# Sliding-window attention with value products on column halves, in an order written out by hand

## The chip, the cores and the metric

The kernel runs on one core of one Trainium2 chip. The metric is the device time of one execution in microseconds, as the median of several runs. The profile comes from one further execution with the hardware profiler on. The engines are named as the profile names them: PE (TensorE, matmuls), PEld (its weight loads), DVE (VectorE), ACT (ScalarE), POOL (GpSimd), and SP (SyncE, which only issues transfers).

## The reference

One step of a two-layer encoder on 2048 prompt tokens and 32 sample tokens, in float32. Layer A is a gated delta rule with eight heads. From its output x one shared K and V (4 heads of 64) are projected. Layer B is attention in chunks of 64 tokens: each chunk reads its own keys and those of the two chunks before it, 16 query heads in groups of four share one K/V head, and a learned sink takes part in the softmax.

```
q = rope(x @ w_q) * 64**-0.5 ;  z = x @ w_z
s = q . k                                   # own chunk and two back, <= 192 keys
m = max(s.max(-1), sink)
p = exp(s - m) ;  p = p / (p.sum(-1) + exp(sink - m))
out = (p @ v * silu(z)) @ w_out             # 1024 x 1024
y = layer_norm(ALPHA * x + out)
```

The 32 sample tokens read a cache of 128 keys and their own 32 in the same way. The change touches layer B's attention and what stands just before it.

## The kernel before

The program runs through layer A, then through `P2`, the projection of x onto K, V, Q and the gate z, then through `Attention`. What matters here is P2 and the attention.

**P2.** Weights were split beforehand into a high and a low part, and a product is three matmuls for each of four slices of 128 rows (`product`, L1291 to L1293), 12 matmuls of 416 columns. Ten units (V, K, and four each of Q and z) are worked on three spans of tokens: tokens 0 to 415 in the plain way, four products per unit (`plain`), and two spans of 832 tokens with seven Winograd-like products per unit (`winograd`, reading tiles named xs). `units` is a generator that yields after each product, and `sequence` fixes the order of units. Weights come through a ring of 12 tiles (`load`, L1273, issued from ACT's queue); `load` is called after each product and fills the ring again. Splitting the sums of x for a span (`load_pair`, L1189, L1194, L1215) is interleaved with plain units: `both` takes two pieces of the split for each product. What follows a product (tanh gate for z, rope for Q and K, transposition for V) is queued in `todo` and worked off later by `after`.

**Attention, per chunk of 64 tokens** (`chunk`), for each of two pairs of K/V heads (p = 0, 1):

- Scores, L1624: four f32 matmuls. Two heads share the 128 partitions, 64 each, so a matmul uses only 64 rows of the array, the lower or the upper.
- Softmax: maximum on DVE (L1499, L1500, L1508), four exponentials with their sums on ACT (L1507, L1509), reciprocal on DVE (L1510, L1511), scaling on POOL (L1632). The scaled sets lie with two heads side by side for each key chunk.
- Turning, L1639: six transposes through PE into tiles tr, copied back by ACT (L1641) and DVE (L1643) as pt.
- Values, L1645: three matmuls of 256 columns. The stationary operand is vd, the values of one chunk for two heads on a block diagonal, half of it zeros. The result is multiplied by the gate (L1648).

vd is loaded from memory in four pieces for each stretch of chunks (L1488), around memsets on POOL (L1486). Two chunks make a tile of 128 tokens, whose output projection and norm are `finish`: 48 matmuls of 512 columns (L1532 to L1534), layer norm on DVE, ACT and POOL. Chunks go in the order 10 to 31, then 0 to 9, and the sample last (`sample`).

**What sets the order.** P2 up to the last Winograd unit stands in a block in which PE, DVE, ACT and POOL work in the order written. Attention stands outside it: there the planner of the language orders all engines by its own estimate of costs. The last four plain units are given out with the first four chunks, and 16 pieces of output weights are loaded afterwards by `open_right`, when the memory of P2 is free.

Of the kernel before, what the change touches and what calls it, by code (L numbers as in the profile page):

```python
# [1134 lines left out]
class P2:  # L1135
# [10 lines left out]
    def __init__(self, tc, right, mid, I, O, T, G):  # L1146
        self.tc, self.nc, self.I, self.O, self.T, self.G = tc, tc.nc, I, O, T, G
        self.res = new_pool(tc, right, "p2_res", 1, side="right")
        self.wp = new_pool(tc, right, "p2_w", self.RING, side="right")
# [3 lines left out]
        self.ppl = None  # L1153
        self.turn = 0
        self.todo, self.second, self.staged = [], [], []
# [3 lines left out]
    def load_right(self):  # L1159
# [20 lines left out]
        for t, c in zip(self.cs0, ("cos", "sin")):  # L1180
            nc.sync.dma_start(t[:], self.I[c][:, 0:TB])

# [83 lines left out]
    def load(self, most=2):  # L1266

        for _ in range(most):
            if self.loads and len(self.held) < self.RING:
                what, slot = self.loads.pop(0)  # L1270
                w = self.wp.tile([128, 2, 4, 128], F32R, tag="w", name="w")
                src = self.T["w2"][UNITS.index(what[:2]), SLOTS.index(slot)]
                self.nc.scalar.dma_start(w[:].rearrange("p s k c -> p s (k c)").bitcast(F32), src)  # L1273
# [10 lines left out]
    def spare(self):  # L1284
        return self.wk.tile([128, 4, 128], F32, tag="hT", name="hT", bufs=2)

    def product(self, ps, w, x, first, last):
        nc = self.nc
        for k in range(4):
# [5 lines left out]
    def units(self, units):  # L1295

        self.loads = [(u, s) for u in units for s in self.slots(u)]
        self.held = []
# [20 lines left out]
    def plain(self, unit):  # L1319
# [3 lines left out]
        for c in range(2):  # L1323
            ps = (self.ppl or self.ppr).tile([128, 512], F32, tag="ps", name="ps")[:, :TB]
            for h in range(2):
                self.product(ps, self.weight(unit, self.PLAIN[c][h]), x[4 * h:4 * h + 4], h == 0, h == 1)
# [111 lines left out]
class Attention:  # L1438


    def __init__(self, tc, left, I, O, T, G):
# [9 lines left out]
        self.turn = 0  # L1451
# [3 lines left out]
        self.nsk = one.tile([128, 8], F32, tag="nsk", name="nsk")  # L1455
        self.sks = one.tile([128, 4], F32, tag="sks", name="sks")
        for i in range(2):
            nc.sync.dma_start(self.nsk[i * 64:i * 64 + 64, :], I["sinks"][i].partition_broadcast(64))
        for i in range(4):
            nc.sync.dma_start(self.sks[i * 32:i * 32 + 32, :], I["sinks_s"][i].partition_broadcast(32))  # L1460
        V.tensor_scalar(out=self.nsk[:], in0=self.nsk[:], scalar1=-1.0, scalar2=None, op0=ALU.mult)
        V.tensor_scalar(out=self.sks[:], in0=self.sks[:], scalar1=-1.0, scalar2=None, op0=ALU.mult)
        self.pend = []
        self.data = {}

    def open_right(self, right):
        tc, I = self.tc, self.I
        R = "right"
        self.oone = new_pool(tc, right, "u_one", 1, side=R)
        self.otwo = new_pool(tc, right, "u_two", 2, side=R)  # L1470
        self.pp = new_pool(tc, right, "u_pp", 1, PSUM, side=R)
        self.ps_s.append(new_pool(tc, right, "u_ps", 1, PSUM, side=R))
        rest = load_out_weights(self.nc, self.oone, self.T["wo"][1], self.nc.sync)
        self.w = next(rest)
        drain(rest)

    def tables(self):
        self.tabs = ln_tables(self.nc, self.oone, self.I["b_ln_g"], self.I["b_ln_b"])

    def load_kv(self, a, z):  # L1480
        nc, T = self.nc, self.T
        nc.sync.dma_start(self.kT[:, :, a * 64:z * 64], T["bk"][:, :, a * 64:z * 64].rearrange("a p t -> p a t"))
        src = T["bv"][0:NP, :].rearrange("(c k) (p d) -> k c p d", k=64, p=2)
        for i in range(2):
            rows, off = slice(i * 64, i * 64 + 64), slice(64 - i * 64, 128 - i * 64)
            nc.gpsimd.memset(self.vd[rows, a:z, :, off], 0.0)  # L1486
            for p in range(2):
                nc.sync.dma_start(self.vd[rows, a:z, p, rows], src[:, a:z, p, rows])  # L1488

    def scores_tile(self):  # L1490
        self.turn += 1
        return self.ps_s[self.turn % len(self.ps_s)].tile([128, 2, 2, 256], F32, tag="S", name="S")

    def softmax(self, S, P, nskc):

        nc, V, thr = self.nc, self.nc.vector, self.thr
        nsub = len(P)
        nm = thr.tile([128, 4], F32, tag="nm", name="nm")
        V.tensor_reduce(out=nm[:, :nsub], in_=S, axis=AX.X, op=ALU.max, negate=True)  # L1499
        V.tensor_tensor(out=nm[:, :nsub], in0=nm[:, :nsub], in1=nskc, op=ALU.min)  # L1500
        sm = thr.tile([128, 4], F32, tag="sm", name="sm")
        es_ = thr.tile([128, 4], F32, tag="es", name="es")
        for u in range(nsub):
            src = S[:, u, :]
            if len(P[u].shape) == 3:
                src = src.rearrange("r (j k) -> r j k", k=64)
            nc.scalar.activation(P[u], src, AF.Exp, bias=nm[:, u:u + 1], scale=1.0, accum_out=sm[:, u:u + 1])  # L1507
# [428 lines left out]
```

## Time and profile before

| | us |
|---|---|
| median of 3 runs | 2197.37 |
| range of the runs | 2195.75 to 2205.4 |
| the profiled execution | 2203.02 |
| its span, first to last instruction | 2201.2 |
| PE busy | 2103.0 (96%) |
| DVE busy | 1490.1 (68%) |
| ACT busy | 911.1 (41%) |
| POOL busy | 713.5 (32%) |

Times inside the profile are microseconds from the start of the span. The attention begins near 1762 and takes the rest. A row of the timeline gives start, length, engine, line, operation, operands and count; starts are measured, while the ends of matmuls are modelled, so the cost of a matmul in a stream is read from one start to the next. Stretches list for each engine its busy time and its count of instructions.

### The profile page before, as it was taken

The numbers are of one execution on the slowest core, as the hardware profiler recorded it, in microseconds if no ns is written. First come the engines' busy times: TensorE is split into PE (matmuls) and PEld (weight loads), VectorE is DVE, ScalarE is ACT, GpSimd is POOL, SyncE is SP. The second block draws the span as 40 slices with busy tenths as digits, with TensorE's granted clock in tenths as the row PEclk, the third lists the DMA queues.
The fourth block names the chain that finished last, engine by engine and source line by source line (L and its number), as shares of the span: only waits on it lengthen the run. The fifth ranks groups of instructions, "written<-read, shape, count | busy, mean of one in ns | idle before, by whom it ended". The sixth has DMA issues, their size and how long they took to land.

```text
span 2201.2 us, 37188 instructions
## 1 busy us (share of the span) xinstructions
PE 2103.0 (96%) x13370; PEld 1911.1 (87%) x13370; DVE 1490.1 (68%) x2771; ACT 911.1 (41%) x2405; POOL 713.5 (32%) x1176
## 2 busy tenths in 40 slices
PE   8999999999989999998889999899899988999997
PEld 6999999999989889887778888899899976888775
DVE  5888977876657589888865665555835566556663
ACT  5545545544422477667742111311311034444441
POOL 1212211161111188788841210000000025565653
PEclk9999999999999999999999999999999999999999
DMA  7656656567764645545735766888788895333321
GB/s 283 224 186 192 223 172 195 175 191 242 243 212 161 204 131 163 153 147 180 235 105 179 255 218 243 298 278 284 266 285 285 273 305 135 100 83 96 96 73 43
DMA packets 348377, 430.00 MB, mean 195 GB/s; under 512 B 78352, under 2 KB 276080, under 8 KB 348176
## 3 DMA queue, kind: packets, MB, share of 16 engines
q1 hardware_dynamic: 311856, 311.07, 44.5%
q10 hardware_dynamic: 36336, 116.55, 15.8%
q8 instruction: 106, 1.74, 0.3%
q14 instruction: 79, 0.65, 0.1%
HBM read 269.45 MB, written 158.44 MB: 194 GB/s over the span
## 4 chain that ended last, share of the span: by engine, by line
PE 77%; DVE 9%; POOL 5%; ACT 4%; DMA 3%; issue 2%; ACTq 0%; SPq 0%; POOLq 0%; DVEq 0%
PE ps L77 10%; PE ps L79 10%; PE ps L78 10%; PE ps L1291 5%; PE ps L1292 5%; PE ps L1293 5%; PE ot L1645 3%; PE po L1052 3%; PE po L1054 3%; PE po L1053 3%; PE po L1532 3%; PE po L1533 3%; PE po L1534 3%; PE S L1624 2%; POOL Tt L588 2%
## 5 line engine op out<-in xcount | busy, mean ns | idle before, releaser
L77 PE MATMUL ps<-act_hi,w_hi 128*128 128x416 f32 x1280 | 458.7, 358 | 6.4 <-DVE z L322 2.7
L79 PE MATMUL ps<-act_hi,w_lo 128*128 128x416 f32 x1280 | 450.5, 353 | 5.0 <-POOL w_lo L54 3.2
L78 PE MATMUL ps<-act_lo,w_hi 128*128 128x416 f32 x1280 | 451.3, 353 | 0.0
L77 PEld LDWEIGHTS ps<-act_hi,w_hi 128*128 128x128 f32 x1280 | 241.8, 189 | 11.0 <-DVE z L322 3.1
L79 PEld LDWEIGHTS ps<-act_hi,w_lo 128*128 128x128 f32 x1280 | 242.0, 189 | 9.8 <-POOL w_lo L54 4.3
L78 PEld LDWEIGHTS ps<-act_lo,w_hi 128*128 128x128 f32 x1280 | 242.6, 190 | 2.8
L1291 PE MATMUL ps<-xs_h,w 128*128 128x416 f32 x560 | 199.6, 356 | 11.4 <-DVE ra L1348 7.1
L1292 PE MATMUL ps<-xs_l,w 128*128 128x416 f32 x560 | 199.9, 357 | 3.1 <-DVE xs_l L1194 3.1
L1293 PE MATMUL ps<-xs_h,w 128*128 128x416 f32 x560 | 198.4, 354 | 0.0
L54 POOL TENSOR_TENSOR w_lo<-w_raw,w_hi 128x1024 fp32r<-128x1024 f32 x32 | 80.5, 2516 | 357.3 <-ACT w_hi L53 343.3
L295 DVE SCALAR_TENSOR_TENSOR y<-R,convw,y 128x2083 f32<-128x2083 f32 (+2 forms) x78 | 175.1, 2245 | 24.8 <-ACT y L293 24.6
L585 POOL TENSOR_TENSOR tm<-L,Tt 128x60 f32<-128x60 f32 (+19 forms) x375 | 136.3, 363 | 87.9 <-DVE L L572 49.9
L588 POOL TENSOR_TENSOR Tt<-Tt,tm 128x60 f32<-128x60 f32 (+19 forms) x375 | 143.6, 383 | 28.3
L1632 POOL TENSOR_TENSOR P<-P,sm 128x384 f32<-128x384 f32 (+2 forms) x128 | 100.9, 810 | 119.1 <-DVE sm L1511 56.5
L1486 POOL MEMSET vd<- 64x768 f32 (+2 forms) x10 | 7.8, 778 | 397.0 <-DVE ra L1348 396.7
L1507 ACT ACTIVATE P<-S,nm 128x192 f32<-128x192 f32 (+2 forms) x260 | 104.6, 419 | 61.1 <-DVE nm L1500 52.3
L1291 PEld LDWEIGHTS ps<-xs_h,w 128*128 128x128 f32 x560 | 106.4, 190 | 14.6 <-DVE ra L1348 7.8
L1348 DVE SCALAR_TENSOR_TENSOR ra<-ps,u 128x416 f32<-128x416 f32 x60 | 35.4, 590 | 122.3 <-PE ps L1293 121.4
L1052 PE MATMUL po<-wo,g_hi 128*128 128x512 f32 (+1 forms) x272 | 110.7, 407 | 0.9 <-DVE hT L1100 0.9
L1292 PEld LDWEIGHTS ps<-xs_l,w 128*128 128x128 f32 x560 | 106.2, 190 | 5.6 <-DVE xs_l L1194 4.2
L1293 PEld LDWEIGHTS ps<-xs_h,w 128*128 128x128 f32 x560 | 106.9, 191 | 1.2
L95 ACT CAST pre_hl<-pre_raw 128x256 fp32r<-128x256 f32 x184 | 65.7, 404 | 101.6 <-DMA pre_raw<-in_b_w_z 25.8
(298 smaller groups left out, 4799.8 us busy)
## 6 DMA issues: line engine op xcount, KB each, us to landing
w<-s_w ACTq DMA_DIRECT2D x180, 512.0 KB, 4.6
s_w<-pre_hl SPq DMA_DIRECT2D x160, 256.0 KB, 2.5
w_raw<-in_w_in SPq DMA_DIRECT2D x32, 512.0 KB, 6.5
s_wo<-pre_hl SPq DMA_DIRECT2D x64, 256.0 KB, 4.1
gb<-s_gcum SPq DMA_DIRECT2D x34, 256.0 KB, 5.2
k<-s_k SPq DMA_DIRECT2D x34, 256.0 KB, 4.0
s_z<-z SPq DMA_DIRECT2D x40, 208.0 KB, 2.1
s_q<-y SPq DMA_DIRECT2D x8, 1024.0 KB, 5.2
```

The source lines that it names most:

```text
L77: nc.tensor.matmul(ps, hi[:, k, :], xh[:, k, :], start=(k == 0), stop=False)
L78: nc.tensor.matmul(ps, hi[:, k, :], xl[:, k, :], start=False, stop=False)
L79: nc.tensor.matmul(ps, lo[:, k, :], xh[:, k, :], start=False, stop=(k == KC - 1))
L295: self.nc.vector.scalar_tensor_tensor(out=y[:, a:z], in0=R[:, a + j:z + j], scalar=self.convw[:, i, j:j + 1], in1=y[:, a:z], op0=ALU.mult, ...
L585: P.tensor_tensor(out=tm[:n, i0 - k:, :w], in0=L[:n, i0:, j:j + 1].to_broadcast(sh), in1=Tt[:n, j:j + 1, :w].to_broadcast(sh), op=ALU.mult)
L588: P.tensor_tensor(out=Tt[:n, i0:, :w], in0=Tt[:n, i0:, :w], in1=tm[:n, i0 - k:, :w], op=ALU.subtract)
L1052: nc.tensor.matmul(ps[:n], ghi[:, k, :n], w[0][k][:, cs], start=(k == 0), stop=False)
L1291: nc.tensor.matmul(ps, w[:, 0, k], xh[:], start=first and k == 0, stop=False, skip_group_check=True)
L1292: nc.tensor.matmul(ps, w[:, 0, k], xl[:], start=False, stop=False, skip_group_check=True)
L1293: nc.tensor.matmul(ps, w[:, 1, k], xh[:], start=False, stop=last and k == 3, skip_group_check=True)
L1507: nc.scalar.activation(P[u], src, AF.Exp, bias=nm[:, u:u + 1], scale=1.0, accum_out=sm[:, u:u + 1])
L1632: nc.gpsimd.tensor_tensor(out=P[:, u, :nj], in0=P[:, u, :nj], in1=f.unsqueeze(1).unsqueeze(3).to_broadcast([128, nj, 2, 64]), op=ALU.mult)
```

## The change

The pieces of `chunk` become methods that are called one by one, in an order written out by hand for PE, DVE and ACT (POOL and SP stay with the planner):

- `scores(n)`: all eight score matmuls of a chunk, then both maxima. `exps`, `norm`, `turn`, `values` are the other steps.
- For `norm` and `turn`, the keys of a chunk are a pair (two chunks that lie together in 128 partitions of the new tile vp) and a single chunk. The sets of a pair are turned as four blocks of 128 keys, one for each query pair and head; the single's two heads lie side by side in P1 and are turned together.
- `values`: for the pair, two matmuls with 64 stationary columns, one for each head, into the lower and the upper 64 output partitions; for the single, two more with the halves of vd. Four matmuls of 256 columns for each head pair, where there were three.
- `beside(n)`: scores of chunk n, then turning of the chunk before it between quarters of a half tile of output projection, then that chunk's values. `first` does it for the first chunk after P2, and `opening` for the first four, between halves of the plain products (`fine`).
- The sample stands between chunk 31 and chunk 0, as one step of this order.
- vp is loaded in one transfer per stretch; the diagonal blocks of vd are copied from it by POOL.
- The ring of weights moves to a place of its own that outlives P2. After the last projection weights it takes 12 of the 16 output weight pieces; four are loaded as before.
- Keys of chunks 8 to 11 (kTa), queries of chunks 10 to 13 and the sinks are loaded during P2 into a place of their own.
- In the sequence of P2 units, z 3 for tokens 0 to 415 moves ahead of the first Winograd span (ten plain products there instead of six), and V for these tokens moves ahead of the second span. Three plain units instead of four are left beside the attention.
- The last tile is stored in halves on two queues. The norm of a tile is issued within the next tile's projection. A buffer for turned rows of layer A's output shares the tag rs.

```diff
     def __init__(self, tc, ring, right, mid, I, O, T, G):
+        self.wp = new_pool(tc, ring, "p2_w", self.RING, side="right")
+        self.kp = new_pool(tc, ring, "p2_keep", 1, side="right")
...
+    def first_keys(self):
+        src = self.T["bk"][:, :, 512:768].rearrange("a p t -> p a t")
+        self.nc.sync.dma_start(self.keep[1][:], src)
+        self.queries(10)
+        self.queries(12)
...
     def spare(self):
-        return self.wk.tile([128, 4, 128], F32, tag="hT", name="hT", bufs=2)
+        return self.wk.tile([128, 4, 128], F32, tag="rs", name="hT")
...
-        self.loads = [(u, s) for u in units for s in self.slots(u)]
+        self.loads = [(u, s) for u in units for s in self.slots(u)] + [(None, i) for i in range(self.RING)]
...
 class Attention:
-        self.ps_s = [new_pool(tc, left, "t_ps", 1, PSUM, side=L)]
-        self.ps_t = new_pool(tc, left, "t_pt", 2, PSUM, side=L)
+        self.ps_s = new_pool(tc, left, "t_ps", 2, PSUM, side=L)
+        self.ps_t = [new_pool(tc, left, "t_pt", 1, PSUM, side=L)]
...
+        self.ps_t.append(new_pool(tc, right, "u_pt", 1, PSUM, side=R))
...
+    def load_v(self, a, z):
+        both = T["bv"][a * 64:z * 64, :].rearrange("(c k) d -> k c d", k=128)
+        nc.sync.dma_start(self.vp[:, a // 2:z // 2, :], both)
+        for h in range(2):
+            rows, off = slice(h * 64, h * 64 + 64), slice(64 - h * 64, 128 - h * 64)
             nc.gpsimd.memset(self.vd[rows, a:z, :, off], 0.0)
+            for odd in range(2):
+                src = self.vp[odd * 64:odd * 64 + 64, a // 2:z // 2, :].rearrange("k b (p h d) -> k b p h d", p=2, h=2)
+                nc.gpsimd.tensor_copy(self.vd[rows, a + odd:z:2, :, rows], src[:, :, :, h])
...
+    def turn(self, n, p):
+        src += [(c, P[:, c, at:at + 128]) for c in range(4)]
+        src += [(4 + u, single[:, u].rearrange("r h k -> r (h k)")) for u in range(2)]
+        for copy in (nc.scalar.copy, V.tensor_copy):
+            now, src = src[:3], src[3:]
+            tr = self.turn_tile()
+            for i, (_, a) in enumerate(now):
+                nc.tensor.transpose(tr[:, i, :], a, ident[:, :])
+            copy(pt[:, c:c + len(now), :], tr[:, :len(now), :])
+            yield
...
+    def values(self, n):
+        ot = self.ps_o.tile([128, 2, 256], F32, tag="ot", name="ot")
+        for p in range(2):
+                    for h in range(2):
+                        hs = slice(h * 64, h * 64 + 64)
+                        nc.tensor.matmul(ot[hs, p], self.vp[:, pair, p * 128 + h * 64:p * 128 + h * 64 + 64],
+                                         pt[:, 2 * h:2 * h + 2, :], start=True, stop=one is None)
+                    for h in range(2):
+                        hs = slice(h * 64, h * 64 + 64)
+                        nc.tensor.matmul(ot[hs, p], self.vd[:, one, p, hs], pt[:, 4:6, :],
+                                         start=pair is None, stop=True)
...
+    def opening(self, chunks):
+        for n in chunks:
+            self.scores(n)
+            self.exps(n, 0)
+                for i, step in enumerate(itertools.chain(self.turn(self.prev, 0), self.turn(self.prev, 1))):
+                    if i == 1:
+                        self.exps(n, 1)
+                    yield
+                    if i >= 2:
+                        self.norm(n, i - 2)
+                yield
+                self.values(self.prev)
...
+    def beside(self, n):
+        m, self.prev = self.prev, n
+            self.scores(n)
+            self.exps(n, 0)
+        next(self.out)
+        drain(self.turn(m, 0))
+            self.exps(n, 1)
+            self.norm(n, 0)
+        next(self.out)
+        drain(self.turn(m, 1))
+            self.norm(n, 1)
+        next(self.out)
+        next(self.out)
+        self.values(m)
...
-    pairs = [("v", 0), ("z", 0), ("k", 0), ("z", 1), ("q", 0), ("z", 2), ("q", 1), ("z", 3), ("q", 2), ("q", 3)]
-    sequence = [("z", j, 0) for j in range(3)] + [p + (1,) for p in pairs]
-    sequence += [("z", 3, 0), ("k", 0, 0), ("q", 0, 0)] + [p + (2,) for p in pairs]
-    sequence += [("q", j, 0) for j in range(1, 4)] + [("v", 0, 0)]
+    pairs = [("v", 0), ("z", 0), ("k", 0), ("q", 0), ("z", 1), ("q", 1), ("z", 2), ("q", 2), ("q", 3), ("z", 3)]
+    sequence = [("z", j, 0) for j in range(4)] + [p + (1,) for p in pairs]
+    sequence += [("v", 0, 0), ("k", 0, 0), ("q", 0, 0)] + [p + (2,) for p in pairs]
+    sequence += [("q", j, 0) for j in range(1, 4)]
...
-        both(itertools.islice(late, 6), p2.load_pair(1))
+        both(itertools.islice(late, 10), p2.load_pair(1))
...
-        drain(itertools.islice(late, 70))
+        drain(itertools.islice(late, 35))
+        p2.first_keys()
+        drain(itertools.islice(late, 35))
         p2.rest()
...
+    order = list(range(10, 32)) + ["s"] + list(range(10))
+    with tc.manual_schedule(engines={ET.PE, ET.DVE, ET.Activation}):
+        for i, _ in enumerate(att.opening([order.pop(0) for _ in range(4)])):
+            drain(itertools.islice(late, 1))
+        drain(late)
+        p2.rest()
+        right.close()
+        att.open_right(right, p2.out)
+        att.first(order.pop(0))
+        att.load_k(0, 8)
+        att.load_v(0, 8)
+        for n in order:
+            att.beside(n)
+        att.rest()
```

More of the change, by code (lines that the diff above doesn't have):

```diff
@@ L1462, in __init__, with open_right @@
[L1462 to L1467, printed above, removed]
+        self.vp = one.tile([128, 16, 256], F32, tag="vp", name="vp")
+        self.qs, self.kTa, self.nsk, self.sks = keep
+        self.pend, self.todo, self.prev = [], [], None
+        self.data, self.probs, self.turned = {}, {}, {}
+        self.late = False
+    def open_right(self, right, pieces):
+        nc, tc = self.nc, self.tc
@@ L1516, in finish, with rest, ready @@
+    def rest(self):
+        self.beside(None)
+        self.late = True
+        drain(self.out)
+        for f in self.todo:
+            f()
+    def ready(self):
+        nc, pool = self.nc, self.otwo
+        t0, n, graw = self.pend.pop(0)
         r = pool.tile([128, D], F32, tag="r", name="r")
```

447 lines of the change are left out of this document (267 added, 180 removed).

## The prediction

> **What bounds the kernel now.** I read the page's busy shares first.
>
> ```profile
> PE 2103.0 (96%) x13370; PEld 1911.1 (87%) x13370; DVE 1490.1 (68%) x2771; ACT 911.1 (41%) x2405; POOL 713.5 (32%) x1176
> ```
>
> TensorE sets the end. Because its ends are modelled, busy time alone hides slack, so next I read the stretches of the last 840 us (columns: stretch, length, busy and count of PE, PEld, DVE, ACT, POOL, granted clock, DMA share, GB/s).
>
> ```profile
> 1379.70:1395.70 16.00, 8.63 (x26) 6.45 (x25) 14.69 (x30) 8.88 (x19) 0.00 (x0) 0.68 0.84 285
> 1762.00:1855.40 93.40, 80.50 (x475) 66.22 (x474) 59.59 (x139) 39.09 (x164) 31.93 (x37) 1.00 0.88 245
> 1855.40:2128.00 272.60, 272.19 (x1492) 216.14 (x1488) 167.05 (x398) 127.83 (x487) 166.25 (x154) 1.00 0.32 90
> 2166.05:2192.00 25.95, 24.35 (x96) 14.47 (x96) 4.83 (x12) 3.42 (x3) 11.73 (x9) 0.93 0.12 41
> ```
>
> The reader is to see four places: a join before the first Winograd units where PE starts only 26 matmuls in 16 us; the opening of the attention, short of work for PE and full in DMA (share 0.88); a long steady part where PE is never idle; and an end part at clock 0.93. In the steady part only fewer or cheaper matmuls help, so their prices come from start to start, from the timeline of PE there:
>
> ```profile
> 1950.71 1.46 PE L1645 MATMUL ot<-pt,vd 128*128 128x256 f32 x6
> 1952.00 0.82 PE L1639 MATMUL tr<-ident,P 128*128 128x128 f32 x6
> 1952.58 0.48 PE L1533 MATMUL po<-wo,g_hi 128*128 128x512 f32 x1
> 1952.89 0.39 PE L1534 MATMUL po<-wo,g_lo 128*128 128x512 f32 x1
> ...
> 1954.95 0.40 PE L1534 MATMUL po<-wo,g_lo 128*128 128x512 f32 x1
> 1955.28 0.92 PE L1624 MATMUL S<-kT,qs 64*128 64x192 f32 x8
> 1956.13 0.70 PE L1645 MATMUL ot<-pt,vd 128*128 128x256 f32 x2
> ...
> 1958.28 0.60 PE L1624 MATMUL S<-kT,qs 64*128 64x192 f32 x4
> 1958.81 0.50 PE L1532 MATMUL po<-wo,g_hi 128*128 128x512 f32 x1
> 1959.15 0.39 PE L1533 MATMUL po<-wo,g_hi 128*128 128x512 f32 x1
> ```
>
> Each f32 matmul has two records. Output projection: 1952.89 to 1954.95 in 9 steps, **0.229** each. Values: 6 records in 1.29, **0.215** each, 12 per chunk: 2.58. Transposes: 6 in 0.58, and the first matmul behind them takes 0.31 (0.08 more): 0.66 per head pair, 1.32 per chunk. Scores: 8 records 0.85, 4 records 0.53, so 0.32 per four and **0.21 fixed** for leaving the row halves; entering costs 0.33 instead of 0.23 (0.10), the first matmul after it 0.34 (0.11): 1.06 per head pair, 2.12 per chunk. Sum 6.02 per chunk beside the projection. The counts agree (tile po, then tile graw, in the steady stretch):
>
> ```profile
> 1855.40:2128.00 272.60, 147.89 (x577) 104.21 (x577) 16.48 (x24) 1.00 0.32 90
> 1855.40:2128.00 272.60, 19.79 (x47) 12.73 (x12) 28.55 (x12) 1.00 0.32 90
> ```
>
> 577 x 0.229 = 132.1 leaves 140.5 us for 47 half chunks: **5.98 per chunk**.
>
> **The change, part by part.** *Values on column halves.* Per head pair, three full products become four with 64 stationary columns: two over 128 keys of two chunks, two over the single chunk. 16 records per chunk instead of 12; all hangs on whether both halves stream at once. The nearest row is the triangular inverse, whose L696 writes the two 64-column halves in turn from the same 64 rows:
>
> ```profile
> 794.06 0.68 PE L696 MATMUL bps<-ta,npr 64*64 64x64 f32 x16
> 794.67 0.66 PE L612 MATMUL vtr<-ident,v 128*128 128x128 f32 x4
> ```
>
> 16 records in 0.61. One after the other, at a quarter of the 0.215 of 256 columns, they would need 0.86 before any change of form, so halves do overlap. Bounds for one chunk: 16 x 0.215 = 3.44 serial, 8 x 0.215 = 1.72 paired. I take paired plus one lone slot, since a matmul's second record must follow its first: 1.94. The Trainium skill (TensorE: Matmul & The Clock Gate, Measured speedup vs the span model) gives 2.38 for three column tiles; by that efficiency two would take 3.44/1.59 = 2.16, an estimate, which would add some 6 us over 28 chunks; L696's row does not separate the two.
>
> *Changes of form.* Before, scores stood in two groups per chunk; after, both head pairs go in one group right behind the previous chunk's values. Rows for such a change are in the sample's values:
>
> ```profile
> 2155.89 0.40 PE L1534 MATMUL po<-wo,g_lo 128*128 128x512 f32 x1
> 2156.21 0.43 PE L1591 MATMUL ot<-pt,vc 128*64 128x128 f32 x2
> 2156.57 0.43 PE L1592 MATMUL ot<-pt,vn 32*64 32x128 f32 x2
> ```
>
> Two records of 128 columns (0.215) take 0.36 when the form changes behind them: 0.15. Into halves: 0.32 against 0.23, 0.10, and 0.05 in the first step. After: values 1.94 + 0.15 = 2.09; scores 4 x 0.32 + 0.15 in + 0.21 + 0.11 out = 1.75; transposes 1.32. **5.16 per chunk, 0.82 less**; 23.5 chunks in the steady stretch: **19 us** (bounds: 1.2 per chunk, 28, without lone slot and entry; -0.7, so -16, if serial). The Trainium skill (TensorEngine Tiling (Array Packing), Key Properties) says that changing the mode drains the engine, which speaks against a change that adds the column mode; the trace agrees, at 0.10 to 0.15 each. With the drain of some 128 cycles in the Trainium skill (TensorE: Matmul & The Clock Gate, Part 2), an estimate of 0.05 per change, the sum would be about 8 us better than by the rows.
>
> *Fixed order.* PE, DVE and ACT now go as written, so a late producer stops PE with no filler. Durations in the steady stretch:
>
> ```profile
> L1499 DVE TENSOR_REDUCE nm<-S 128x4 f32<-128x768 f32 (+2 forms) x47 | 43.0, 916 | 6.3 <-PE S L1624 6.3
> L1507 ACT ACTIVATE P<-S,nm 128x192 f32<-128x192 f32 (+2 forms) x185 | 74.2, 419 | 37.9 <-DVE nm L1500 29.2 <-PE S L1624 4.7 <-PE tr L1639 1.9
> L1632 POOL TENSOR_TENSOR P<-P,sm 128x384 f32<-128x384 f32 (+2 forms) x92 | 71.5, 799 | 58.6 <-DVE es L1508 35.2 <-DVE sm L1511 23.1 <-DMA qs<-s_bq 0.3
> L1641 ACT COPY pt<-tr 128x384 f32<-128x384 f32 (+2 forms) x47 | 22.0, 467 | 82.8 <-PE tr L1639 82.6
> ```
>
> From the start of a chunk's scores: the previous gating (2 x 0.42, from 19.79/47), then two reductions (0.92 each, with small operations) done at about 3.6; the first is done at 2.3, so four exponentials (4 x 0.42 and a small one) at 4.3, the first copy of turned sets 4.8, the next exponentials 6.7, the second copy 7.2. PE meanwhile has 1.75 scores, four quarter steps of the projection (6 x 0.229 = 1.37 each) and 1.32 transposes: it comes to the values at 8.6. That leaves 1.4 for the cast g_hi or the norm's pass on ACT, each once per tile. The scaled sets (POOL, 3.2 per chunk) are wanted one chunk later. Queries and gates keep two buffers and the planner's order on SP, so their loads still go out a pair ahead; were one stuck behind a store of y, the scores and all behind them on PE would wait. So nothing in the steady part: the cover is 1.4 us, and what exceeds it would be paid 28 times.
>
> *Opening* (1762 to 1855.4). The counts of tiles S, tr and ot there, and PE's longest wait:
>
> ```profile
> 1762.00:1855.40 93.40, 15.20 (x136) 10.67 (x136) 15.22 (x16) 26.25 (x123) 1.00 0.88 245
> 1762.00:1855.40 93.40, 12.61 (x78) 9.09 (x78) 7.19 (x13) 6.26 (x13) 1.00 0.88 245
> 1762.00:1855.40 93.40, 18.49 (x72) 12.91 (x72) 5.02 (x12) 1.00 0.88 245
> PE S L1624 <- ACT P L1507: 8.8, 7, 2.4
> ```
>
> At after's prices: 136 score records are 8.5 chunks x 1.75 = 14.9, 78 transposes 6.5 x 1.32 = 8.6, 72 value records 6 x 2.09 = 12.5, one tile of projection 48 x 0.229 = 11.0. The other 141 of 475 are plain projection, 0.19 each by the start-to-start rows below: 26.8. Sum 74 of 93.4, **19 us lost** today.
>
> ```profile
> 1767.27 0.35 PE L1292 MATMUL ps<-x_l,w 128*128 128x416 f32 x1
> 1767.46 0.35 PE L1293 MATMUL ps<-x_h,w 128*128 128x416 f32 x1
> ```
>
> After, keys 8 to 11 and queries 10 to 13 are in place, plain products come in halves of 1.13 between the pieces, and 12 of 16 pieces of the output weights follow the projection weights through the ring. What stays: one bank for turned sets, so the second group waits for the first copy, which stands on ACT behind four exponentials: ready at 4.5 from the scores, wanted at 3.2. With rope work ahead of the reductions I take 3 us per chunk for three chunks, 2 for the first chunk after them, 1 to 2 for the last four weight pieces, which can start only when the projection's tiles are free. That is 11 to 12, so **8 us** gained (bounds 19 and 0). ACT's ring transfers wait for a slot, that is for a product; exponentials and copies queue behind, but PE has passed that product already. The V unit moves from here into the covered middle: 9.0 on PE in both places, zero. The early keys and queries (1.25 MB) go beside Winograd matmuls; uncovered they cost some 4 us at 285 GB/s. On-chip copies put 8192 elements per partition on POOL; at the 799 ns per 384 of the scaling that is at most 17 us, most of it in the opening, where POOL is busy 31.9 of 93.4. The sinks' small loads and the shared turning buffer hide behind full PE.
>
> *Join.* Ten plain steps instead of six stand ahead of the first Winograd unit, the splits spread over the first six as before. 26 matmuls x 0.19 = 4.9 of 16.0: **11 us** lost today, waits 7.4 and the rest a clock of 0.68:
>
> ```profile
> PE ps L1291 <- ACT xs_h L1189: 4.3, 2, 4.0
> PE ps L1292 <- DVE xs_l L1194: 3.1, 3, 1.5
> ```
>
> Four more steps are 48 x 0.19 = 9.0 of cover, which exceeds the waits: I take **9** (bounds 0 and 11). The second join, behind rope work, keeps its order.
>
> *End.* The last two tiles, 96 x 0.229 = 22.0 against 25.95, have no sample beside them: 3. In the last chain POOL's rsqrt stood behind the previous tile's norm:
>
> ```profile
> 2192.16 2.33 POOL L1545 TENSOR_TENSOR r<-r,ln_b 32x1024 f32<-32x1024 f32 x1
> 2193.22 0.21 DVE L1538 BATCH_NORM_AGGREGATE mv<-st 128x2 f32<-128x12 f32 x1
> ...
> 2194.47 0.65 POOL L466 TENSOR_SCALAR ln_y<-mv 128x1 f32<-128x1 f32 x1
> ```
>
> 1 us of that, 1 for the chunks just before: **5**.
>
> **Sum:** 19 + 8 + 9 + 5 = 41. The profiled execution took 2203.0 (span 2201.2 and 1.8 around it), 5.6 above the median of 2197.4: 2162 for it, **2156 on the median**.
>
> **Rivals.** *The halves run one after another* (the change wouldn't do what it says): 1.5 per chunk more over 30 chunks, 45: 2201. L696 speaks against it, though with 64 rows. *The fixed order stalls* (slower): PE waits in every chunk for the copy behind the exponentials, as here before, with no projection to fill:
>
> ```profile
> 1798.64 0.92 PE L1624 MATMUL S<-kT,qs 64*128 64x192 f32 x8 [1.08 <-ACT P L1507]
> ```
>
> 1.08 per half chunk, 2.16 x 28 = 60: 2216; it decides from 41/28 = 1.5 per chunk. The 5.5 us of projection between scores and values speak against it. *Opening and join keep their losses:* 17 more, 2173. *The opening has no waits:* 12 less, 2144.
>
> **How the numbers follow.** Forecast 0.58, no waits 0.12, losses kept 0.15, serial 0.05, stalls 0.10. Range 2135 (steady 27, opening 19, join 11, end 5) to 2185 (steady 12, nothing else); it leaves out serial and stalls. Half a per cent, 11 us, is about what a measurement tells from no change. Faster: 0.58 + 0.12 + 0.15 = 0.85; same: serial and the mildest stalls, 0.07; slower 0.08.
>
> **What would show it.** Value groups of 16 records lasting about 2.1 us (3.6 would be serial); a tile of projection every 21.3 us (two chunks of 5.16 and 48 x 0.229) instead of 22.9; PE without waits between the opening and the end; no clock below 1 near 1385; waits on turned sets in the opening. A steady part with PE waiting on pt or P would make it wrong.

## The result, and the profile after

The changed kernel takes **2181.0 us** (median of 11 runs, 2174.2 to 2194.0) against 2199.9 for the kernel before in the same series (2194.9 to 2205.4): a ratio of **0.9914, 95% interval 0.9895 to 0.9932**, 19 us less. The forecast was 41 less, 2156. The profiled executions give 2201.2 and 2179.6 us of span, 21.6 less. So the sign is right and the size is under half.

First the busy shares of the changed kernel:

```profile
PE 2068.7 (95%) x13494; PEld 1874.1 (86%) x13494; DVE 1477.4 (68%) x2767; ACT 906.8 (42%) x2405; POOL 725.1 (33%) x1194
```

Then four stretches of it that answer those shown of before (columns as there): the join, the opening up to the first matmul of the output projection, the twelve groups of 48 projection records that follow the first tile (eleven tiles and the sample), and the last two tiles.

```profile
1387.50:1403.50 16.00, 11.05 (x48) 9.85 (x47) 9.58 (x19) 6.85 (x15) 0.00 (x0) 0.87 0.86 291
1757.90:1823.40 65.50, 48.64 (x309) 41.09 (x309) 39.92 (x93) 24.56 (x103) 34.66 (x48) 0.89 0.85 271
1844.60:2106.70 262.10, 249.15 (x1595) 183.55 (x1593) 162.23 (x409) 124.85 (x498) 164.25 (x150) 1.00 0.34 91
2146.70:2171.40 24.70, 23.14 (x98) 17.83 (x96) 5.43 (x11) 3.43 (x3) 13.44 (x9) 1.00 0.23 85
```

PE still sets the end, with 1% less of the span. It was never idle in the steady part before (272.19 of 272.60). Now it is idle for 13.0 of 262.1 us there. In the opening it is idle for 16.9 of 65.5 at a clock of 0.89, where before, up to the same point, it was 11.1 of 71.6 at 1.00:

```profile
1757.90:1829.50 71.60, 60.54 (x362) 51.24 (x360) 45.29 (x108) 27.72 (x112) 21.75 (x28) 1.00 1.01 294
```

What PE waits for, by the waits of the changed kernel (engine, tile and line waited for: us in total, times, longest). The first two rows are of the opening, the next two of the steady part, the next three of the join, the last of the end.

```profile
PE tr L1670 <- ACT pt L1672: 11.5, 4, 6.7
PE tr L1670 <- POOL P L1627: 5.3, 1, 5.3
...
PE tr L1670 <- ACT pt L1672: 11.9, 11, 1.4
PE tr L1653 <- DVE pt L1656: 1.1, 1, 1.1
...
PE ps L1330 <- DVE ra L1391: 3.3, 1, 3.3
PE ps L1330 <- ACT xs_h L1223: 1.2, 1, 1.2
PE ps L1331 <- DVE xs_l L1228: 0.5, 1, 0.5
...
PE S L1818 <- DVE r L1823: 1.6, 2, 0.8
```

A chunk in the steady part, from PE's timeline (start, length, tile, records). Column halves: 16 value records from 1929.82 to 1931.70.

```profile
1926.25 0.85 PE L1670 MATMUL tr<-ident,P 128*128 128x128 f32 x6 [1.02 <-ACT pt L1672]
...
1929.82 0.65 PE L1695 MATMUL ot<-pt,vp 128*64 128x256 f32 x4
1930.30 0.60 PE L1700 MATMUL ot<-pt,vd 128*64 128x256 f32 x4
1930.73 0.60 PE L1695 MATMUL ot<-pt,vp 128*64 128x256 f32 x4
1931.17 0.60 PE L1700 MATMUL ot<-pt,vd 128*64 128x256 f32 x4
1931.70 1.57 PE L1597 MATMUL S<-kT,qs 64*128 64x192 f32 x16
1933.20 0.50 PE L1818 MATMUL po<-w,g_hi 128*128 128x512 f32 x1
...
1940.28 0.65 PE L1695 MATMUL ot<-pt,vp 128*64 128x256 f32 x4
```

Values **1.88** (forecast 2.09), scores 1.50 (1.75). From values to values, 1929.82 to 1940.28, a chunk without a wait takes **10.46**, where the forecast's prices make 10.66 (5.16 and 24 x 0.229). The prices were right, if anything too high; the Trainium skill's efficiency (TensorE: Matmul & The Clock Gate, Measured speedup vs the span model), weighed in the prediction at 2.16 for the values, doesn't fit this trace. But every other chunk has the wait in the first row, so that a tile takes **22.15**, not 21.3.

Where the time went, between marks that both traces have: the last Winograd product (at 1757.7 in both), the 48th projection record, 576 records later, the end. "Work" is the difference in records by tile up to each mark, at the changed kernel's prices; in the opening, say, 22 plain projection records, 8 transposes of V, 24 of S, 18 of tr and one chunk of values fewer, 11.4 us.

| stretch | forecast gain | before | after | work in it | gain on equal work |
|---|---|---|---|---|---|
| up to the last Winograd product (join) | 9 | 1757.7 | 1757.7 | 5.1 more | 5, of it 3.6 of PE's idle time |
| opening | 8 | 97.6 | 86.7 | 11.4 less | about -0.5 |
| 576 projection records (steady) | 19 | 272.5 | 262.1 | some 1.7 more | 12 |
| the rest (end) | 5 | 73.2 | 72.9 | some 3.9 more | 4 |

Three of the four terms are short, and the experiments take them in turn. All variants below are the changed kernel with one edit, unless said otherwise; each ratio is against the kernel before on the same chip, so 0.9914 is the value to compare with, and 0.001 is 2.2 us.

### The profile page after: what moved, and what is told of

The parts are those of the page before. It is cut to its first block, busy times and chain, and to the rows that moved or that the text cites. A ratio compares the mean times of both kernels' runs of the same rounds, so it can differ in the third digit from the quotient of the medians.

```text
span 2179.6 us, 37384 instructions
## 1 busy us (share of the span) xinstructions
PE 2068.7 (95%) x13494; PEld 1874.1 (86%) x13494; DVE 1477.4 (68%) x2767; ACT 906.8 (42%) x2405; POOL 725.1 (33%) x1194
## 3 DMA queue, kind: packets, MB, share of 16 engines
q10 hardware_dynamic: 38208, 123.10, 16.9%
q8 instruction: 107, 1.75, 0.3%
## 5 line engine op out<-in xcount | busy, mean ns | idle before, releaser
L77 PEld LDWEIGHTS ps<-act_hi,w_hi 128*128 128x128 f32 x1280 | 242.0, 189 | 10.1 <-DVE z L322 4.3
L295 DVE SCALAR_TENSOR_TENSOR y<-R,convw,y 128x2083 f32<-128x2083 f32 (+2 forms) x78 | 175.1, 2245 | 24.5 <-ACT y L293 24.3
L1627 POOL TENSOR_TENSOR P<-P,sm 128x512 f32<-128x512 f32 (+2 forms) x126 | 101.7, 831 | 87.8 <-DVE sm L1624 69.2
```

Source lines behind the costliest of these rows:

```text
L77: nc.tensor.matmul(ps, hi[:, k, :], xh[:, k, :], start=(k == 0), stop=False)
L295: self.nc.vector.scalar_tensor_tensor(out=y[:, a:z], in0=R[:, a + j:z + j], scalar=self.convw[:, i, j:j + 1], in1=y[:, a:z], op0=ALU.mult, ...
L1627: nc.gpsimd.tensor_tensor(out=out, in0=part, in1=f, op=ALU.mult)
```

## Experiments

### The steady wait: a cast ahead of a copy

In the second chunk of each tile ACT's timeline reads: four exponentials, then the cast g_hi, then the copy that frees the bank of the transposes. DVE's small operation L1604 beside POOL's pass L1836 is the other thing that stands out.

```profile
1946.82 1.05 ACT L1787 CAST g_hi<-graw 128x1024 fp32r<-128x1024 f32 x1
1947.75 0.50 ACT L1672 COPY pt<-tr 128x384 f32<-128x384 f32 x1
...
1944.12 0.89 DVE L1604 TENSOR_TENSOR nm<-nm,nsk 128x4 f32<-128x4 f32 x1
...
1942.62 2.37 POOL L1836 TENSOR_TENSOR r<-r,ln_b 128x1024 f32<-128x1024 f32 x1
```

The copy has ended at 1948.25, and PE's second group of transposes starts at 1948.39, after a wait of 1.02. So the cast (0.93 from start to start) or the 0.73 that L1604 takes beyond its usual 0.16 could be what is late.

```diff
-                if j >= 4 and ahead is None and self.pend:
+                if j >= 6 and ahead is None and self.pend:
```

> The cast g_hi of the next tile (1.05 us on ACT) is issued two quarter steps later, behind both ACT copies of turned sets instead of ahead of them. Theory A (the cast stands on ACT ahead of the copy that frees the bank for the second group of transposes): the wait of 1.0 us once per tile goes, a tile of projection comes every 21.0 to 21.1 us instead of 22.15, 14 tiles, so 14 to 16 us less than the changed kernel, about 2166. Rival B (POOL's passes over r hold up DVE's small operations, so that the exponentials start late whatever ACT does): the wait stays once per tile, within 4 us of the changed kernel.

Measured: **2169.8 us, ratio 0.9852 (0.9833 to 0.9872)**, some 13.7 less than the changed kernel. The stretch of the same 576 projection records, and behind it PE's waits in it:

```profile
1849.90:2101.30 251.40, 248.76 (x1594) 183.56 (x1592) 158.58 (x409) 124.87 (x498) 164.23 (x150) 1.00 0.35 95
```

```profile
PE tr L1670 <- ACT pt L1672: 1.8, 2, 1.0
```

251.4 against 262.1 and, before, 272.5: 21 us less than before, where 19 were forecast for this part. A tile takes 21.18. Theory A holds; beyond two chunks of 10.46 a tile keeps 0.26, which the stretched small operation of rival B would explain (not tested alone). Two waits stay, in the tiles after the sample.

### Do the column halves need to take turns?

```diff
-                if pair is not None:
-                    for h in range(2):
-                        hs = slice(h * 64, h * 64 + 64)
+                for h in range(2):
+                    hs = slice(h * 64, h * 64 + 64)
+                    if pair is not None:
                         nc.tensor.matmul(ot[hs, p], self.vp...)
-                if one is not None:
-                    for h in range(2):
-                        hs = slice(h * 64, h * 64 + 64)
+                    if one is not None:
                         nc.tensor.matmul(ot[hs, p], self.vd...)
```

> The four value products of a head pair are issued with both products of one column half first, then both of the other, instead of the halves in turn. Same work, same output. Theory A (two products on different column halves stream at the same time only as direct neighbours; with this order only one pair of records in four overlaps or none): 16 records take 2.8 to 3.4 us instead of 1.88, 0.9 to 1.6 per chunk, 30 to 50 us more than the changed kernel, 2210 to 2230, above the kernel before. Rival B (a product of 64 columns is cheaper by itself, or the engine finds the overlap in any order): within 3 us of the changed kernel.

Measured: 2184.0, **0.9916 (0.9898 to 0.9935)**: the same. Theory A fell. PE's timeline of this variant:

```profile
1932.04 0.66 PE L1695 MATMUL ot<-pt,vp 128*64 128x256 f32 x4
1932.52 0.61 PE L1698 MATMUL ot<-pt,vd 128*64 128x256 f32 x4
1932.96 0.65 PE L1695 MATMUL ot<-pt,vp 128*64 128x256 f32 x4
1933.39 0.65 PE L1698 MATMUL ot<-pt,vd 128*64 128x256 f32 x4
1933.97 1.57 PE L1597 MATMUL S<-kT,qs 64*128 64x192 f32 x16
```

1.93 for the 16 records. In the program the first half's products (L1695, L1698) stand ahead of the second half's, yet by their starts all four records of L1695 come before the four of L1698: the second half's first record starts 13 ns behind the first half's first, which stands four places ahead of it. So the halves do stream at the same time, and PE finds this over a distance of four records.

### The join

```diff
-    sequence = [("z", j, 0) for j in range(4)] + [p + (1,) for p in pairs]
-    sequence += [("v", 0, 0), ("k", 0, 0), ("q", 0, 0)] + [p + (2,) for p in pairs]
+    sequence = [("z", j, 0) for j in range(3)] + [p + (1,) for p in pairs]
+    sequence += [("z", 3, 0), ("v", 0, 0), ("k", 0, 0), ("q", 0, 0)] + [p + (2,) for p in pairs]
...
-        both(itertools.islice(late, 10), p2.load_pair(1))
+        both(itertools.islice(late, 6), p2.load_pair(1))
...
-        drain(itertools.islice(late, 21))
+        drain(itertools.islice(late, 25))
```

> The fourth z unit (four plain steps) goes back from ahead of the first Winograd units to the plain units before the second ones, so that six plain steps stand there as in the kernel before; the opening of the attention is as in the changed kernel. Theory A (as predicted: the steps cover waits that are otherwise lost): 9 us more than the changed kernel, about 2190. Rival B (the splits are a chain on DVE of about 26.6 us, 1369.6 to 1396.2, whose end sets when the second Winograd product can go on, and the added steps' own copies and gates queue behind the splits on ACT and DVE): 2 to 4 us more.

Measured: 2184.2, 0.9919 (0.9903 to 0.9935): 1 us more by the ratios, within what can be told apart; between the first and the last Winograd product, less the 48 more plain records (9.1), 372.1 against 370.1. The edit moves the unit and does not remove it: at the first join PE's waits are 8.4 instead of 5.0, at the second, where the unit now stands, 4.2 instead of 5.9. So the term is worth 2 to 4, not 9. Rival B names a cause: DVE works on the splits from 1369.6 to 1396.2, before from 1367.4 to 1397.0, whatever stands on PE. PE's third wait (3.3, on ra) is for a sum that stands on DVE behind all of them and behind the gates:

```profile
1397.10 0.59 DVE L1446 SCALAR_TENSOR_TENSOR a<-zs,a 128x416 f32<-128x416 f32 x1 [0.39 <-ACT zs L1445]
1398.93 0.59 DVE L1446 SCALAR_TENSOR_TENSOR a<-zs,a 128x416 f32<-128x416 f32 x1 [1.24 <-DMA w<-s_w]
1399.44 0.58 DVE L1391 SCALAR_TENSOR_TENSOR ra<-ps,u 128x416 f32<-128x416 f32 x1
```

Around that wait DVE itself is idle for 1.6: the gates need ACT's part (L1445), which stands on ACT among copies and issues of weights. Is it the splits' order or their amount? Two more edits: spread the twelve portions over all ten plain steps, and move twelve subtractions to idle POOL.

```diff
-    def both(a, b):
+    def both(a, b, twice=99):
...
-        for _ in a:
-            drain(itertools.islice(b, 2))
+        for i, _ in enumerate(a):
+            drain(itertools.islice(b, 2 if i < twice else 1))
...
-        both(itertools.islice(late, 10), p2.load_pair(1))
+        both(itertools.islice(late, 10), p2.load_pair(1), 2)
```

> At the first join the splits' twelve portions are issued over all ten plain steps (two, two, then one each) instead of over the first six, so that the z units' copies and gates stand between them instead of behind them all. Theory A (the 3.3 us wait of the second Winograd product is order: its sum waits on DVE behind the gates that wait behind the splits): that wait goes below 1 us, the two before it grow by less than 1, 2 to 3 us less than the changed kernel. Rival B (it is DVE's amount of work, the same in any order): within 1 us.

```diff
-            self.low("P7", k, b12, V)
+            self.low("P7", k, b12, nc.gpsimd)
...        (the same for P5 and P4)
```

> Twelve of the 28 low parts of each pair's splits (of P7, P5 and P4) are subtracted on POOL, idle at the joins, instead of DVE. Theory A (the join is bound by DVE's chain of splits, 26.6 us of it back to back): DVE has 6 us less, PE's waits of 1.2, 0.5 and 3.3 us at the first join and 3.3 at the second go to under 2 together, 4 to 6 us less than the changed kernel. Rival B (DVE and POOL hold each other up, as when L1468 took 2.73 us instead of 0.58 beside g_lo): DVE's subtractions and sums beside POOL's stretch by as much as is moved, and the time is the same within 2 us or longer.

Spread: 2181.3, 0.9904 (0.9883 to 0.9925), 2 less by the ratios, not to be told from the changed kernel: the wait on ra fell from 3.3 to 1.3, the first rose from 1.2 to 1.9, and the three together fell from 5.0 to 3.7. So order is a part of it; the times don't decide between the theories, and that the rest is DVE's amount of work isn't shown. On POOL: 2191.3, **0.9949 (0.9931 to 0.9968)**, 8 slower. The groups by line of DVE at the join, the changed kernel first, then this variant's DVE and POOL (count, busy, mean ns):

```profile
L1228 DVE TENSOR_TENSOR xs_l<-b,xs_h 128x416 fp32r<-128x416 f32 x28 | 15.5, 585 | 2.9 <-ACT xs_h L1223 2.8
L1249 DVE TENSOR_TENSOR b<-b,b 128x416 f32<-128x416 f32 x16 | 9.3, 583 | 0.0
L1446 DVE SCALAR_TENSOR_TENSOR a<-zs,a 128x416 f32<-128x416 f32 x6 | 3.5, 585 | 1.6 <-DMA w<-s_w 1.2 <-ACT zs L1445 0.4
```

```profile
L1249 DVE TENSOR_TENSOR b<-b,b 128x416 f32<-128x416 f32 x16 | 12.7, 805 | 0.2
L1228 DVE TENSOR_TENSOR xs_l<-b,xs_h 128x416 fp32r<-128x416 f32 x16 | 11.1, 732 | 1.7 <-ACT xs_h L1223 1.7
L1446 DVE SCALAR_TENSOR_TENSOR a<-zs,a 128x416 f32<-128x416 f32 x4 | 4.5, 1136 | 2.1 <-ACT zs L1445 2.1
...
L1228 POOL TENSOR_TENSOR xs_l<-b,xs_h 128x416 fp32r<-128x416 f32 x12 | 15.4, 1306 | 25.7 <-ACT xs_h L1223 25.7
```

Twelve operations went from DVE to POOL, and DVE's remaining ones grew from 583 to 805, from 585 to 732 and, the gates, from 585 to 1136 ns. POOL's work holds DVE's up. That DVE holds POOL up isn't shown: POOL's subtractions take 1.09 to 1.49 us whether DVE works beside all of one or beside a third of it.

### The opening

First the part that was meant to help: undo the place for the first keys and queries.

```diff
-                if 10 <= n < 12:
-                    kT, k0 = self.kTa, k0 - 512
...
-        p2.first_keys()
```

> The place of their own for the first keys and queries isn't used: keys 8 to 11 come from the common key tile and queries 10 to 13 are loaded when the first chunks start, through SP at the opening. Theory A (as predicted: this part of the change took 2.4 to 8.8 us of waits for the first scores out of the opening): 5 to 9 us more than the changed kernel. Rival B (the opening's chain through ACT, DVE and POOL is longer than the loads, so that scores later by some us only move the waits): within 2 us.

Measured: 2187.7, 0.9936 (0.9916 to 0.9956), 4.8 more than the changed kernel by the ratios, whose intervals still overlap; the opening of the profile is 71.3 instead of 65.7, with a wait of 7.3 for the keys' transfer ahead of the scores. Theory A: this part gains. The loss comes from what follows. ACT and DVE of the changed kernel, ahead of PE's wait of 5.3 (to 1773.46):

```profile
1768.81 0.33 ACTq L1308 DMA_DIRECT2D w<-s_wo  x1
1769.19 0.52 ACT L1373 ACTIVATE a<-ps 128x416 f32<-128x416 f32 x1 [4.63 <-DMA s_bz<-ra]
...
1775.94 0.52 ACT L1373 ACTIVATE a<-ps 128x416 f32<-128x416 f32 x1 [6.24 <-DMA w<-s_wo]
...
1769.74 0.61 DVE L1465 STREAM_SHUFFLE rs<-a 128x416 f32<-128x416 f32 x1
...
1771.40 0.16 DVE L1623 TENSOR_TENSOR sm<-sm,es 128x4 f32<-128x4 f32 x1
```

ACT stands 4.6 and then 6.2 us in front of issues of pieces of output weights (L1308) until earlier transfers have landed; the copy a, DVE's rope, the sums sm behind rope and POOL's scaling P follow. Ahead of the wait of 6.7 (to 1822.24) the reductions for the fifth chunk stand on DVE behind the last rope, one pass of which is stretched while POOL subtracts g_lo:

```profile
1815.38 2.73 DVE L1468 TENSOR_TENSOR a<-a,cos 128x416 f32<-128x416 f32 x1
...
1815.19 2.47 POOL L1788 TENSOR_TENSOR g_lo<-graw,g_hi 128x1024 fp32r<-128x1024 f32 x1 [3.08 <-ACT g_hi L1787]
```

Three edits, each for one cause: the pieces issued from SP; the first chunk's sums early; the fifth chunk's scores early.

```diff
-                    self.nc.scalar.dma_start(flat.bitcast(F32), self.T["wo"]...)
+                    self.nc.sync.dma_start(flat.bitcast(F32), self.T["wo"]...)
```

> The 12 pieces of the output weights that follow the projection weights through the ring are issued from SP's queue instead of ACT's; nothing else moves. Theory A (ACT, in order, stands 4 to 6 us at a time in front of such an issue until an earlier transfer has landed, and rope, reductions, exponentials and copies stand behind it): PE's waits of 5.3, 2.1 and 6.7 us in the opening shrink to 1 to 2 each, 10 us less than the changed kernel, about 2171. Rival B (the opening is bound by its transfers, DMA share 0.98 in the first half, whoever issues them): the loss of about 28 us stays within 3, and the scores may wait for queries that SP issues late.

```diff
-                for _ in range(5):
-                    yield
-                self.norm(n, 0)
-                self.norm(n, 1)
-                yield
+                for i in range(6):
+                    yield
+                    if i == 1:
+                        self.norm(n, 0)
+                        self.norm(n, 1)
```

> In the first chunk of the opening the sums and reciprocals (and with them POOL's scaling) are issued after two quarter steps instead of five, so that they stand on DVE ahead of the rope passes that wait for ACT. Theory A (the wait of 5.3 us on P is order: P's sums behind rope, rope behind ACT, ACT behind a transfer): the wait goes to under 1.5 us and the clock drop behind it too, 4 to 7 us less than the changed kernel. Rival B (POOL, busy with 25 of 36 us of copies of values there, is late by itself, or the same wait comes back at the next copy): 0 to 2 us less.

```diff
+    def begin(self, n):
+        self.scores(n)
+        self.exps(n, 0)
     def first(self, n):
         m, self.prev = self.prev, n
+        drain(self.turn(m, 0))
         got = self.ready()
         self.out = self.outs(got)
-        self.scores(n)
-        self.exps(n, 0)
-        drain(self.turn(m, 0))
...
         drain(late)
+        att.begin(order[0])
         p2.rest()
```

> At the end of the opening, the scores and the first four exponentials of the fifth chunk are issued before the last query unit's rope work instead of behind it, and the first cast g_hi moves behind the first copy of turned sets; the work is the same. Theory A (PE's longest wait of 6.7 us stands there because the reductions are queued on DVE behind rope passes, one of which POOL's subtraction g_lo stretched from 0.58 to 2.73 us): that wait shrinks to 2 to 3 us, 4 us less than the changed kernel. Rival B (ACT blocked in front of a transfer is what holds the copy): the wait stays at 5 to 7, within 1 us of the changed kernel.

| edit | us | ratio (95% interval) | opening, us | with the first tile, us | PE's long waits in the opening |
|---|---|---|---|---|---|
| none (changed kernel) | 2181.0 | 0.9914 (0.9895 to 0.9932) | 65.7 | 86.9 | 5.3, 2.1, 6.7 |
| pieces from SP | 2178.9 | 0.9897 (0.9879 to 0.9916) | 62.9 | 85.1 | 2.0, 3.2, 6.3 |
| sums early | 2185.8 | 0.9924 (0.9907 to 0.9942) | 67.4 | 89.2 | 8.0, 6.7 |
| scores early | 2182.9 | 0.9910 (0.9894 to 0.9926) | 63.8 | 88.1 | 5.0, 3.1, 2.2 |

(Opening: from the start of the last Winograd product to that of the first projection matmul; with the first tile: to that of the second tile's first.) None gains alone what its wait was, and none's time is clear of the changed kernel's. Early sums took the wait of 5.3 away and it came back as 8.0 at the next copy, which stands on ACT behind the next issue: rival B of that run. Early scores cut 6.7 to 2.2, 1.3 and 0.8, but the first tile then took 24.3 instead of 21.2 at a lower clock. The three and the late cast together; then the same with the pieces back on ACT; then all four, with the fourth chunk's first transposes ahead of the fifth chunk's scores:

> Late cast, output-weight pieces from SP, the fifth chunk's scores ahead of the last rope and the first chunk's sums early, all in one. Theory A (the losses are orders on DVE and ACT that stand one behind the other): steady 14 less as measured, opening 10 to 14 less than the changed kernel: about 2155, what was forecast. Rival B (the opening is bound by its transfers, 0.98 of their share in its first half): only the steady part's 14 and the last wait's 4, about 2163.

> As the run with all four edits, but the output-weight pieces stay on ACT's queue. Theory A (ACT standing in front of a transfer is a cause of its own): 4 to 6 us more than with all four, about 2169. Rival B (with sums and scores early nothing on PE's path waits behind ACT's issues): within 1.5 us of the run with all four.

> As the run with all four edits, and the fourth chunk's first transposes stand ahead of the fifth chunk's scores, so that their copy on ACT is ahead of the exponentials. Theory A (the last waits, 2.2 and 1.3 us, are order, and the low clock after them goes with them): 3 to 5 us less than with all four, about 2160. Rival B (the output projection that follows then waits for its last pieces of weights, whose transfers end when they end): within 1.5 us.

All four edits: **2164.6, 0.9827 (0.981 to 0.9844)**, 38 less than before and faster than both kernels. Its opening, and behind it the largest of PE's waits on ACT, in the opening, and on weights, in the first tile:

```profile
1760.80:1815.60 54.80, 45.84 (x309) 38.14 (x308) 39.17 (x92) 24.56 (x103) 32.27 (x46) 1.00 0.97 306
```

```profile
PE tr L1670 <- ACT pt L1672: 5.7, 4, 2.2
PE po L1821 <- DMA wo<-s_wo: 1.6, 2, 0.8
PE po L1820 <- DMA wo<-s_wo: 1.0, 1, 1.0
```

The same 309 PE records in 54.8 instead of 65.5, at clock 1.00 instead of 0.89 and a DMA share of 0.97. The three edits alone add up to 3.0 us of the opening (2.8 less, 1.9 less, 1.7 more); together they take 10.7 out of it. But about half of that comes back at once: the first tile takes 26.4 instead of 21.2, and PE waits there for the last pieces of its weights (the last two rows above, and a stretch of that tile):

```profile
1822.00:1827.00 5.00, 2.46 (x6) 0.98 (x5) 0.00 (x0) 0.00 (x0) 0.00 (x0) 0.89 0.89 320
```

With the first tile it is 81.4 against 86.9: 5.6 less, where the three alone add up to 1.6 more; by the ratios 5.5 less than with the late cast alone, with intervals that just overlap. So the orders stood one behind the other, as theory A says, but the time is near rival B's 2163 and not 2155: part of what the orders free is lost again in front of the last transfers and at a lower clock (0.87 in the first tile, 0.94 in the changed kernel's). With the pieces back on ACT (the second run) it is 2172.2, 0.9862 (0.9842 to 0.9882), the opening 63.8, and the wait of 7.8 on ACT's copy is there again: ACT's standing in front of transfers is a cause of its own, worth 7.7 here. With the transposes ahead of the scores as well (the third) it is 2168.9, 0.9849 (0.9833 to 0.9865): no gain, rival B. There the projection, 0.2 us earlier, waits for g_hi, g_lo and the last pieces of its weights, and its first tile takes 29.0 instead of 26.4.

## Why the prediction was right or wrong

**Column halves, changes of form: right**, a little better than priced (1.88 for 2.09, 1.50 for 1.75). The serial rival is out by the overlapping starts.

**"So nothing in the steady part: the cover is 1.4 us": wrong.** This is the step that cost most, 13.7 us by the late cast. The cover was worked out up to the values, for the cast or the norm's pass on ACT behind the second copy. But what comes due first is the second head pair's group of transposes, which needs the bank that the first copy frees, and that copy stood behind the cast. The fixed-order rival had the right mechanism, an ACT copy too late for PE, at a quarter of its rate: one wait of 1.0 per tile, not 1.08 per half chunk. The step from rows to deadline failed, not the durations. With the cast moved the part gives 21, for 19 forecast.

**Opening, 8 gained: wrong.** Its terms for what stays (three times 3, 2, and 1 to 2) add up to 12 to 13, not to "11 to 12", so that 6 to 7 of gain would have followed; but what stays was mis-sized by much more. 16.9 of idle PE and a clock of 0.89 on 48.6 us of work (some 5 more, an estimate: 48.6 x 0.11) make 22. The clock had no term at all. The 9 for three chunks came out at 10.1, near it by luck: 7.4 in the first chunk (5.3 and 2.1, behind ACT's issues), 1.4 and 1.3 in the others. Two sentences of the prediction failed: that behind ACT's ring transfers "PE has passed that product already" (true of the ring's slot, but the issue also waits for earlier transfers, 4.6 and 6.2 us at a DMA share near 1, and all of ACT behind it), and the 2 us for "the first chunk after them", where rope, stretched by POOL, stood ahead of the reductions: 6.7. The place for keys and queries is worth 4.8 to 5.6 of it.

**Join, 9: wrong.** The step that more cover than the waits takes them all away (9.0 of it, "which exceeds the waits") took the waits for a fixed sum. They are the end of a chain of some 26.6 us on DVE, and the added unit put its own gates, with ACT's part of them, at the end of that chain: a new wait of 3.3 on ra. Worth 2 to 4; how much of what is left is order and how much DVE's work stays open. The sign "no clock below 1 near 1385" failed too: 0.87.

**End, 5: about right**, 4 on equal work; two new waits of 0.8 for DVE's r are part of why the last two tiles take 24.7 instead of 22.0. The forecast "losses kept", 2173, described the opening well and the join in part; the steady wait it didn't have.

## What to carry to other kernels

When an order is fixed by hand, list for each instruction of the side engines the first thing on the bound engine that needs it, banks it frees included, and measure the cover to that, not to the data's last reader. A transfer issued from a computing engine's queue can stop that engine: ACT stood 4.6 and 6.2 us here, at a DMA share near 1; try a queue that computes nothing. Several waits in a row on one chain are taken out together or not at all: three edits worth nothing clear alone were worth 5.5 us in common. And measure past the stretch that was mended: of 10.7 us taken out of the opening, 5.1 came back in the next tile.

## What the runs showed of the hardware

- **Column halves overlap without taking turns**: products on the other half start beside a record four places ahead of them, 16 records in 1.93 us against 1.88.
- **POOL's work holds DVE up**: L1468 took 2.73 us instead of 0.58 beside a POOL subtraction of 2.47; at the join DVE's operations with two tile operands grew by a quarter to almost double beside POOL's of 1306 ns each. TENSOR_REDUCE of a score tile beside L1836 kept its 0.96. The Trainium skill (SBUF — State Buffer, SBUF: two separate sides) has an exclusive lock on a shared pair of ports, taken by DVE operations with two SBUF inputs against a POOL operation that reads SBUF; the trace agrees: L1468 starts 0.19 behind POOL's subtraction and ends 0.45 behind its end.
- **A long wait is paid twice.** The windows of the changed kernel's opening (the clock is the third figure from the end): behind the waits of 5.3 and 2.1 it is low, while those of 1.4 and 1.3 in the next two rows leave it at 1.00:

```profile
1774.00:1782.00 8.00, 5.86 (x21) 5.02 (x20) 4.03 (x9) 4.40 (x20) 7.42 (x14) 0.53 1.05 377
...
1790.00:1800.00 10.00, 8.57 (x57) 7.00 (x57) 7.57 (x19) 4.78 (x21) 3.57 (x4) 1.00 0.49 161
1800.00:1810.00 10.00, 8.71 (x60) 7.53 (x56) 6.50 (x18) 4.77 (x21) 1.61 (x2) 1.00 0.79 206
...
1822.00:1827.00 5.00, 4.76 (x17) 4.09 (x18) 0.98 (x4) 2.17 (x11) 3.22 (x4) 0.60 0.95 357
```

In the last row, behind the 6.7, 4.76 us of PE at 0.60 do the work of 2.9 (an estimate, 4.76 x 0.60).
